# Mixture-of-experts trunk: token rows of seven experts fetched by indirect DMA and transposed, in place of one-hot products

## The chip, the cores and the metric

The kernel runs on one core of one Trainium2 chip. Its metric is the device time of one execution in microseconds, taken as the median of several runs; lower is better. Of the engines, PE (TensorE) does the matrix products, ACT (ScalarE) and DVE (VectorE) do the elementwise work, SP issues the loads, and POOL (GpSimd) is unused before the change.

## The reference

A two-layer trunk over 256 tokens of width 1024 with 256 context tokens. Layer 0 is attention and a dense SwiGLU, layer 1 is a gated convolution and a top-2-of-8 expert SwiGLU. The change lies in the last part:

```python
h = rms_norm(x, norm2_g[layer]) * (1 + sc2) + sh2
logits = (h @ router_w).astype(jnp.float32)
top_vals, top_idx = lax.top_k(logits, TOP_K)
weights = jax.nn.softmax(top_vals, axis=-1)
gates = jnp.sum(jax.nn.one_hot(top_idx, N_EXPERTS) * weights[..., None], axis=-2)
out = gates[..., 0:1] * swiglu(h, w_gate[0], w_up[0], w_down[0])
for e in range(1, N_EXPERTS):
    out = out + gates[..., e:e + 1] * swiglu(h, w_gate[e], w_up[e], w_down[e])
x = x + g2 * out
```

Each expert has three weight matrices of 1024 x 3584 in f32, 44 MB in all; eight experts make 352 MB that must come from memory.

## The kernel before, in words

The kernel ranks the experts by the number of tokens they got. The first five ranks are heavy (up to 128 tokens each), the last three are light (up to 64 tokens). Each expert's hidden width of 3584 is cut into 7 chunks of 512; a chunk needs six loads of 1 MB (two halves each of gate, up and down). The 56 chunks are processed in one fixed order, `chunks`: four heavy ones first, then heavy and light mixed about two to one, four light ones last. So expert 0 starts at step 0, expert 5 (light) at 5, expert 1 at 9, expert 2 at 20, expert 6 (light) at 25, expert 3 at 31, expert 4 at 41, expert 7 (light) at 44.

A step has twelve places p: in places 0 to 7 PE computes gate and up of its own chunk, in places 8 to 11 it computes down of the chunk before. Weights of a heavy chunk are split first: ACT rounds a half to `hi` (L71), DVE computes `lo` = raw - hi (L72), and PE makes three f32r products (L271, L273, L275). Weights of a light chunk are used as they are, in f32, two products side by side (L1319). The program order of every engine is written out by hand: `hook(n, p, f, ...)` puts a piece of work at step n, place p, and `ahead` and `feed` issue loads and conversions a few halves ahead of their use.

All loads are issued by SP, in order, into a ring of 13 buffers of 1 MB each during the experts. A load waits until the readers of the load 13 places earlier are done: the DVE subtraction for a heavy chunk, the PE product for a light one.

Before expert r starts at step n, its tokens are gathered. `choice` on DVE builds a one-hot `os` (token by slot, scaled with the token's RMS factor) at step n-3; `gather` (heavy, two groups of four column blocks, at n-1, places 5 and 8) or `gather_light` (one group, place 5) multiplies the stream `x` with it on PE in f32, which selects, scales and transposes the rows at once. `gathered` applies the modulation and splits the result. At n+2, `slots` transposes an unscaled one-hot `oh` and reads each slot's gate; `scatter` uses the transposed one after the expert's end to add its output to the tokens.

Of the kernel before, what the change touches and what calls it, by code (L numbers as in the profile page):

```python
# [24 lines left out]
CAP = 64  # L25
# [8 lines left out]
def trunk(ctx, tc, i, out, dbg=None):  # L34
    nc = tc.nc
# [22 lines left out]

    ring = [raw1] * 5

    def load(src, n=2048):
        ring.append(ring.pop(0))
        t = ring[-1].tile([128, 2048], F32, name="raw")
        sp.dma_start(t[:, :n], src)
        return t

# [70 lines left out]
    def ahead(split):  # L137

        n = used[0]
        step = 2 if whole[n // 2] else 1  # L140
        upto, k = n, n + step
        while split and k <= most[0] and k // 2 - n // 2 < 11:
            if whole[k // 2]:
                k += 2
            else:
                upto, k, split = k, k + 1, split - 1
        feed(upto)
        used[0] += step
        return ready.pop(n)

    vec = const.tile([128, 29, 8], F32, name="vec")
    cid = const.tile([128, 130], F32, name="cid")
# [1006 lines left out]
    raw5 = ctx.enter_context(pool("raw5", 1))  # L1159
    ring += [raw5]  # L1160
    me = ctx.enter_context(pool("me", 2))

    gts = m1.tile([128, NT, NE], F32, name="gts")
    posr = m1.tile([128, NT, NE], F32, name="posr")
    gtsr = m1.tile([128, NT, NE], F32, name="gtsr")
    perm = m1.tile([128, NE, NE], F32, name="perm")
    cap = m1.tile([128, NE], F32, name="cap")

# [27 lines left out]
    def by_rank(dst, src):  # L1196
        for t in range(NT):
            tmp = m1.tile([128, NE, NE], F32, name="cmp")
            dve.tensor_mul(tmp, perm, src[:, t, None, :].to_broadcast([128, NE, NE]))
            dve.reduce_sum(dst[:, t], tmp, axis=AX.X)  # L1200

    def gates():

        mx = m1.tile([128, NT], F32, name="mx")
        sm = m1.tile([128, NT], F32, name="sm")
        dve.reduce_max(mx, lg, axis=AX.X)
        dve.tensor_sub(gts, lg, mx[:, :, None].to_broadcast([128, NT, NE]))
        act.activation(gts, gts, AF.Exp)
        dve.tensor_mul(gts, gts, sl.bitcast(F32))
        dve.reduce_sum(sm, gts, axis=AX.X)  # L1210
        dve.reciprocal(sm, sm)
        dve.tensor_mul(gts, gts, sm[:, :, None].to_broadcast([128, NT, NE]))
        by_rank(gtsr, gts)
        for u in units:
            u.finish()
        dump("lg", lg)
        dump("gts", gts)
        dump("pos", pos)
# [1 line left out]
    class Expert:  # L1220
        pass

    def choice(E, pos, scaled):

        name = "os" if scaled else "oh"
        n = 2 if E.light and not scaled else 1
        w = CAP if E.light else 128
        c = me.tile([128, NT, 128], F32, name=name, bufs=1)[:, :, 0:n * w]
        for t in range(NT):
            d, io, p = c[:, t], iota[:, 0:w], pos[:, t, E.r:E.r + 1]  # L1230
            if n == 2:
                d, io = d.rearrange("p (n w) -> p n w", n=2), io[:, None, :].to_broadcast([128, 2, w])
            if scaled:
                dve.tensor_scalar(d, io, p, rs[:, t:t + 1], op0=OP.is_equal, op1=OP.mult)
            else:
                dve.tensor_scalar(d, io, p, None, op0=OP.is_equal)
        setattr(E, name, c)

    def gather_light(E):
        E.ps = pm()  # L1240
        for k in range(KD):
            for t in range(NT):
                pe.matmul(E.ps[:, k * CAP:(k + 1) * CAP], x[:, t, k * 128:(k + 1) * 128], E.os[:, t],
                          start=(t == 0), stop=(t == NT - 1))

    def gathered_light(E):
        E.h = me.tile([128, KD, CAP], F32, name="hl", bufs=1)
        w = [128, KD, CAP]
        dve.tensor_mul(E.h, E.ps.rearrange("p (k c) -> p k c", c=CAP), am[:, :, 0:1].to_broadcast(w))
        dve.tensor_add(E.h, E.h, bm[:, :, 0:1].to_broadcast(w))  # L1250
        choice(E, posr, False)

    def gather(E, ks):
        g = ks[0] // 4
# [19 lines left out]
    def gathered(E, ks, h=None):  # L1274
        h = h or modulated_rows(E, ks)
        g, ks = ks[0] // 4, slice(ks[0] % 4, ks[-1] % 4 + 1)
        act.copy(E.eh[g][:, ks], h)
        dve.tensor_sub(E.el[g][:, ks], h, E.eh[g][:, ks].bitcast(F32))
        if g and ks.stop == 4:
            choice(E, posr if E.r else pos, False)  # L1280

    def slots(E):
        E.ps = pm()
        for t in range(NT):
            pe.transpose(E.ps[:, t * 128:(t + 1) * 128], E.oh[:, t], ident)
        for t in range(NT):
            pe.matmul(E.ps[:, S:S + 1], E.oh[:, t], gtsr[:, t, E.r:E.r + 1], start=(t == 0), stop=(t == NT - 1))

    def slotted(E):
        E.ohT = me.tile([128, S], F32R, name="ohT" + "l" * E.light, bufs=2 - E.light)  # L1290
        E.gs = me.tile([128, 1], F32, name="gs" + "l" * E.light, bufs=2 - E.light)
        act.copy(E.ohT, E.ps[:, 0:S])
        act.copy(E.gs, E.ps[:, S:S + 1])

    def flip(C):
        C.ps = pm()
# [53 lines left out]
    def hook(n, p, f, *a):  # L1350
        hooks.setdefault((n, p), []).append((f, a))
# [48 lines left out]
    def down(C, s):  # L1400
# [10 lines left out]
        else:  # L1411
            k = slice(s * 128, (s + 1) * 128)
            mac(E.accs, C.dh[:, k], C.dl[:, k], *halves(ahead(4)), first, end)

    hook(0, 1, ranks)
    hook(0, 3, by_rank, posr, pos)
    hook(1, 1, gates)
    hook(3, 2, gate_rows, 1, 5, (0, 1), g2)
# [66 lines left out]
def spill(tc, i, out, load, pm, acc, me, m1, x, macc, rs, am, bm, pos, gts, cap, g2, iota, ident):  # L1485
# [4 lines left out]
        dve.tensor_sub(p2[:, t], pos[:, t], cap)  # L1490
    for e in range(NE):
        oh = me.tile([128, NT, 128], F32, name="oh", bufs=1)
        os = me.tile([128, NT, 128], F32, name="os", bufs=1)
# [58 lines left out]
def constants():  # L1552
    c = np.zeros((128, C_ATT + C_END), np.float32)
    p = np.arange(128)[:, None]
    j = np.arange(128)[None, :]
    c[:, C_TRI:C_TRI + 128] = p < j
    c[:, C_ATT + C_M0:C_ATT + C_M0 + 128] = np.where(j > p, NEG, 0.0)
    c[:, C_ATT + C_M1:C_ATT + C_M1 + 128] = np.where(j < p, NEG, 0.0)
    c[:, C_IO:C_IO + 128] = j + 1
    half = 32  # L1560
    inv = (np.float32(10000.0) ** (-np.arange(0, half, 2, dtype=np.float32) / np.float32(half))).astype(np.float32)
    t = np.arange(S)
    ang = np.concatenate([(t // 64).astype(np.float32)[:, None] * inv, (t % 64).astype(np.float32)[:, None] * inv], 1)
# [5 lines left out]
    d = np.zeros((128, 130), np.float32)  # L1569
    d[:, 0:128] = p == j  # L1570
    for r in range(2):
        d[r::32, 128 + r] = 1.0
    return c, d
# [58 lines left out]
```

## Time and profile before

| | us |
|---|---|
| three runs | 1404.34, 1409.27, 1409.58 |
| median | 1409.27 |
| profiled execution | 1407.87 |
| its span, first to last instruction | 1406.1 |
| PE busy in the span | 1375.2 (98%) |
| DVE, ACT, POOL busy | 990.2, 791.2, 0.2 |
| read from memory | 467 MB, 333 GB/s over the span |

The profiled execution's time is 1.8 us more than its span; that rest lies outside the instructions. The experts run from about 500 us to the end. A busy time is the union of an engine's instructions; since matmuls overlap, the cost of a group of them is read from the start of its first to the start of the next group.

### The profile page before, as it was taken

How to read it: one execution, taken by the hardware profiler on the slowest of the kernel's cores; microseconds unless marked ns; L12 is line 12 of the kernel's file. 1: busy time of each engine (PE TensorE's matmuls, PEld its weight loads, DVE VectorE, ACT ScalarE, POOL GpSimd, SP SyncE). 2: the span in 40 equal slices, each digit the busy share in tenths (PEclk: the TensorE clock that was granted, in tenths of full speed). 3: DMA queues.
4: the chain of work that ended last, by engine and by line, in shares of the span. 5: the costliest groups of instructions: out<-in, count | busy, mean ns of one | idle time of the engine just before them, and what ended most of it. 6: DMA issues, size and time to landing. Idle time of an engine off the chain costs nothing.

```text
span 1406.1 us, 20577 instructions
## 1 busy us (share of the span) xinstructions
PE 1375.2 (98%) x7764; PEld 1017.2 (72%) x7764; DVE 990.2 (70%) x1341; ACT 791.2 (56%) x1070; POOL 0.2 (0%) x4
## 2 busy tenths in 40 slices
PE   6999999999999999999999999999999999999997
PEld 4776789999899988776666767767667676676742
DVE  4777769788777679776766867767578667676721
ACT  5567674444463378565655755656467566465610
POOL 0000000000000000000000000000000000000000
PEclk9999999999999999999999999999999999999999
DMA  9734678678667779799899999989989999999994
GB/s 372 277 120 141 250 298 301 240 299 301 251 235 261 275 281 351 286 422 382 343 422 421 420 390 383 378 362 376 421 345 421 413 414 363 364 420 370 411 420 167
DMA packets 66060, 469.81 MB, mean 334 GB/s; under 512 B 7328, under 2 KB 7968, under 8 KB 10016
## 3 DMA queue, kind: packets, MB, share of 16 engines
q1 hardware_dynamic: 65952, 468.41, 84.2%
q8 instruction: 63, 1.03, 0.3%
q14 instruction: 45, 0.37, 0.1%
HBM read 467.33 MB, written 1.05 MB: 333 GB/s over the span
## 4 chain that ended last, share of the span: by engine, by line
PE 93%; ACT 3%; DVE 3%; issue 1%; DMA 0%; DVEq 0%; ACTq 0%
PE pm L1319 11%; PE pm L271 9%; PE pm L273 9%; PE pm L275 9%; PE acc L271 8%; PE acc L273 8%; PE acc L275 8%; PE acc L1319 5%; PE pm L927 4%; PE pm L929 4%; PE pm L928 4%; PE pm L1299 2%; PE pm L1261 2%; PE pm L181 1%; PE pm L1339 1%; PE pt L691 1%
## 5 line engine op out<-in xcount | busy, mean ns | idle before, releaser
L72 DVE TENSOR_TENSOR lo<-raw,hi 128x1024 fp32r<-128x1024 f32 x522 | 627.0, 1222 | 124.9 <-ACT hi L71 100.9
L71 ACT ACTIVATE hi<-raw 128x1024 fp32r<-128x1024 f32 x522 | 545.7, 1059 | 246.8 <-PE pm L275 113.6
L271 PE MATMUL pm<-hi,eh 128*128 128x512 f32 x560 | 224.6, 401 | 0.2
L273 PE MATMUL pm<-lo,eh 128*128 128x512 f32 x560 | 219.0, 391 | 1.8 <-DVE lo L72 1.6
L275 PE MATMUL pm<-hi,el 128*128 128x512 f32 x560 | 218.7, 391 | 0.0
L1319 PE MATMUL pm<-raw,hl 128*64 128x512 f32 x672 | 155.6, 599 | 0.0
L927 PE MATMUL pm<-th,hi 128*128 128x256 f32 x480 | 135.1, 281 | 0.0
L928 PE MATMUL pm<-tl,hi 128*128 128x256 f32 x480 | 134.6, 280 | 0.0
L929 PE MATMUL pm<-th,lo 128*128 128x256 f32 x480 | 134.6, 280 | 0.0
L271 PEld LDWEIGHTS pm<-hi,eh 128*128 128x128 f32 x560 | 105.2, 188 | 32.9 <-issue 8.8
L273 PEld LDWEIGHTS pm<-lo,eh 128*128 128x128 f32 x560 | 105.3, 188 | 24.2 <-DVE lo L72 4.1
L275 PEld LDWEIGHTS pm<-hi,el 128*128 128x128 f32 x560 | 105.1, 188 | 22.5
L1319 PEld LDWEIGHTS pm<-raw,hl 128*64 128x64 f32 x672 | 44.1, 136 | 79.8 <-issue 76.6
L927 PEld LDWEIGHTS pm<-th,hi 128*128 128x128 f32 x480 | 90.8, 189 | 1.2 <-issue 0.8
L928 PEld LDWEIGHTS pm<-tl,hi 128*128 128x128 f32 x480 | 90.7, 189 | 0.4
L929 PEld LDWEIGHTS pm<-th,lo 128*128 128x128 f32 x480 | 90.8, 189 | 0.0
L271 PE MATMUL acc<-hi,dh 128*128 128x512 f32 x280 | 88.6, 398 | 0.0
L273 PE MATMUL acc<-lo,dh 128*128 128x512 f32 x280 | 86.5, 390 | 0.0
L275 PE MATMUL acc<-hi,dl 128*128 128x512 f32 x280 | 86.3, 389 | 0.0
L1313 DVE TENSOR_TENSOR sg<-pm,sg 128x512 f32<-128x512 f32 (+1 forms) x56 | 38.5, 688 | 63.0 <-ACT sg L1312 62.7
L1319 PE MATMUL acc<-raw,dT 128*64 128x512 f32 x336 | 78.1, 600 | 0.0
L1312 ACT ACTIVATE sg<-pm 128x512 f32<-128x512 f32 (+1 forms) x56 | 32.7, 585 | 69.5 <-PE pm L1319 66.4
(323 smaller groups left out, 1639.0 us busy)
## 6 DMA issues: line engine op xcount, KB each, us to landing
raw<-in_moe_d_dram SPq DMA_DIRECT2D x112, 1024.0 KB, 10.2
raw<-in_moe_g_dram SPq DMA_DIRECT2D x111, 1024.0 KB, 9.9
raw<-in_moe_u_dram SPq DMA_DIRECT2D x111, 1024.0 KB, 9.3
raw<-in_ada_w_dram SPq DMA_DIRECT2D x48, 1024.0 KB, 6.7
raw<-in_conv_i_dram SPq DMA_DIRECT2D x12, 1024.0 KB, 6.6
raw<-in_ffn_g_dram SPq DMA_DIRECT2D x11, 1024.0 KB, 6.3
raw<-in_ffn_u_dram SPq DMA_DIRECT2D x11, 1024.0 KB, 5.1
raw<-in_ffn_d_dram SPq DMA_DIRECT2D x11, 1024.0 KB, 5.0
```

The source lines that it names most:

```text
L71: act.activation(hi, r, AF.Copy)
L72: dve.tensor_sub(lo, r, hi.bitcast(F32))
L271: pe.matmul(p, hh, wh[j], start=first, stop=False)
L273: pe.matmul(p, hh, wl[j], start=False, stop=False)
L275: pe.matmul(p, hl, wh[j], start=False, stop=last)
L927: pe.matmul(d, hi[:, c], th[:, k], start=(k == 0), stop=False)
L928: pe.matmul(d, hi[:, c], tl[:, k], start=False, stop=False)
L929: pe.matmul(d, lo[:, c], th[:, k], start=False, stop=(k == KD - 1))
L1261: pe.matmul(E.ps[:, k * 128:(k + 1) * 128], x[:, t, kk * 128:(kk + 1) * 128], E.os[:, t], start=(t == 0), stop=(t == NT - 1))
L1312: act.activation(sg, C.g, AF.Silu)
L1313: dve.tensor_mul(sg, C.u, sg)
L1319: pe.matmul(ps[m * CAP:(m + 1) * CAP], lhsT, w, start=first, stop=last, tile_position=(0, m * CAP))
```

## The change

The stream `x` (1 MB) is stored to a buffer `xd` in memory early in the experts (step 1). For experts 1 to 7 the one-hot `oh` is built at n-3 and goes through `slots` at n-2 instead of n+2. `slots` now multiplies it with three columns: the gate, the RMS factor and the token's number. From the third, as an integer, an indirect DMA on POOL's queue fetches the expert's rows (128 of 4 KB, or 64) from `xd` into a buffer taken from the ring of loads, at step n-2, place 4. ACT scales the rows in place at (n-1, 2), and PE transposes them at the places where the gather products stood. Expert 0 keeps the products. `ahead` looks 9 loads ahead at most instead of 11.

```diff
+    def spare():
+        ring.append(ring.pop(0))
+        return ring[-1].tile([128, 2048], F32, name="raw")
     def load(src, n=2048):
-        ring.append(ring.pop(0))
-        t = ring[-1].tile([128, 2048], F32, name="raw")
+        t = spare()
         sp.dma_start(t[:, :n], src)
...
-        while split and k <= most[0] and k // 2 - n // 2 < 11:
+        while split and k <= most[0] and k // 2 - n // 2 < 9:
...
-        by_rank(gtsr, gts)
+        by_rank(slotv[:, :, :, 0], gts)
+        for t in range(NT):
+            dve.tensor_copy(slotv[:, t, :, 1], rs[:, t:t + 1].to_broadcast([128, NE]))
+            dve.tensor_scalar(slotv[:, t, :, 2], cid[:, 130:131].to_broadcast([128, NE]), 128.0 * t, None, op0=OP.add)
...
+    def fetch_rows(E):
+        E.idx = me.tile([128, 1], I32, name="idx")
+        dve.tensor_copy(E.idx, E.v[:, 2:3])
+        w = CAP if E.light else 128
+        E.xg = spare()[0:w, 0:D]
+        nc.gpsimd.indirect_dma_start(out=E.xg, out_offset=None, in_=xd[:, :],
+                                     in_offset=bass.IndirectOffsetOnAxis(ap=E.idx[0:w, 0:1], axis=0))
+    def scale_rows(E):
+        act.activation(E.xg, E.xg, AF.Copy, scale=E.v[0:E.xg.shape[0], 1:2])
+    def turn_rows(E, ks):
+        ...
+        w = E.xg.shape[0]
         E.ps = pm()
-        for k in range(KD):
-            for t in range(NT):
-                pe.matmul(E.ps[:, k * CAP:(k + 1) * CAP], x[:, t, k * 128:(k + 1) * 128], E.os[:, t], ...)
+        for k, kk in enumerate(ks):
+            pe.transpose(E.ps[:, k * w:(k + 1) * w], E.xg[:, kk * 128:(kk + 1) * 128], ident[0:w, 0:w])
...
-            pe.matmul(E.ps[:, S:S + 1], E.oh[:, t], gtsr[:, t, E.r:E.r + 1], start=(t == 0), stop=(t == NT - 1))
+            pe.matmul(E.ps[:, S:S + 3], E.oh[:, t], slotv[:, t, E.r], start=(t == 0), stop=(t == NT - 1))
...
-            hook(n - 3, 10, choice, E, posr, True)
+            hook(n - 3, 10, choice, E, posr)
+            hook(n - 2, 2, slots, E)
+            hook(n - 2, 3, slotted, E)
+            hook(n - 2, 4, fetch_rows, E)
+            hook(n - 1, 2, scale_rows, E)
             if E.light:
-                hook(n - 1, 5, gather_light, E)
+                hook(n - 1, 5, turn_rows, E, range(KD))
...
-                    hook(n - 1, (5, 8)[g], gather, E, ks)
+                    hook(n - 1, (5, 8)[g], turn_rows, E, ks)
...
-        hook(n + 2, 2, slots, E)
-        hook(n + 2, 3, slotted, E)
...
+    def store_rows():
+        for t in range(NT):
+            sp.dma_start(xd[t * 128:(t + 1) * 128, :], x[:, t])
+    hook(1, 0, store_rows)
```

## Rows read from the trace of the kernel before

**Rows 1.** The page's first part: busy time, share of span, instructions of each engine.

```profile
PE 1375.2 (98%) x7764; PEld 1017.2 (72%) x7764; DVE 990.2 (70%) x1341; ACT 791.2 (56%) x1070; POOL 0.2 (0%) x4
```

**Rows 2.** Windows: stretch, its length, busy time by engine, clock, DMA share, GB/s.

```profile
600.00:1375.00 775.00, 773.21 (x3549) 515.07 (x3550) 529.58 (x524) 447.18 (x521) 0.00 (x0) 1.00 0.97 394
700.00:725.00 25.00, 25.00 (x116) 14.82 (x114) 15.86 (x14) 13.01 (x14) 0.00 (x0) 1.00 1.01 422
525.00:550.00 25.00, 25.00 (x117) 20.73 (x116) 24.59 (x25) 21.75 (x25) 0.00 (x0) 1.00 0.95 358
```

**Rows 3.** Waits from 480 us on: who waited for whom, total, times, longest.

```profile
PEld pm L273 <- DVE lo L72: 4.1, 6, 1.0
PEld pm L1319 <- DMA raw<-in_moe_d_dram: 0.9, 3, 0.3
...
SPq L64 <- DVE lo L72: 384.3, 151, 11.4
SPq L64 <- PE pm L1319: 190.9, 39, 9.6
```

**Rows 4.** Timeline of PE at expert 1's gather: start, length, line, tiles, count.

```profile
640.84 2.05 PE L1261 MATMUL pm<-os,x 128*128 128x128 f32 x16
642.82 2.79 PE L1319 MATMUL pm<-raw,hl 128*64 128x512 f32 x12
645.55 2.05 PE L1261 MATMUL pm<-os,x 128*128 128x128 f32 x16
647.36 0.71 PE L271 MATMUL acc<-hi,dh 128*128 128x512 f32 x2
```

**Rows 5.** Timeline of PE at expert 7's gather and 19 us before it.

```profile
1186.49 2.79 PE L1319 MATMUL pm<-raw,hl 128*64 128x512 f32 x12
...
1205.95 3.68 PE L1243 MATMUL pm<-os,x 128*128 128x64 f32 x32
1209.44 0.48 PE L271 MATMUL pm<-hi,eh 128*128 128x512 f32 x1
```

**Rows 6.** Timeline of PE at transposes of hidden tiles: 128 rows twice, 64 rows once.

```profile
520.70 0.60 PE L1299 MATMUL pm<-cid,sg 128*128 128x128 f32 x4
521.05 0.48 PE L271 MATMUL pm<-hi,eh 128*128 128x512 f32 x1
...
606.93 0.46 PE L1299 MATMUL pm<-cid,sg 64*128 64x64 f32 x4
607.32 0.50 PE L271 MATMUL pm<-hi,eh 128*128 128x512 f32 x1
...
638.39 0.66 PE L1299 MATMUL pm<-cid,sg 128*128 128x128 f32 x4
638.97 1.94 PE L1319 MATMUL pm<-raw,hl 128*64 128x512 f32 x8
```

**Rows 7.** Groups by shape: busy, mean ns of one, idle before, releaser.

```profile
L71 ACT ACTIVATE hi<-raw 128x1024 fp32r<-128x1024 f32 x522 | 545.7, 1059 | 246.8 <-PE pm L275 113.6 <-PE pm L928 64.7 <-PE acc L275 56.1
L1234 DVE TENSOR_SCALAR os<-cst,posr,rs 128x128 f32<-128x128 f32 x8 | 2.4, 340 | 0.0
```

**Rows 8.** Timeline of PE around expert 3's gather, from step 29, place 4.

```profile
980.42 0.39 PE L271 MATMUL pm<-hi,eh 128*128 128x512 f32 x1
...
994.57 2.05 PE L1261 MATMUL pm<-os,x 128*128 128x128 f32 x16
```

**Rows 9.** DMA: x's loads (KB each, median us to landing); L64's loads, min/median/max.

```profile
x<-in_x_dram SPq DMA_DIRECT2D x2, 512.0 KB, 4.5
...
DMA to landing us min/median/max: 4.7/8.9/15.8
```

**Rows 10.** Timeline of SP's issues around expert 1's fetch; then a use on PE.

```profile
597.69 0.86 SPq L64 DMA_DIRECT2D raw<-in_moe_d_dram  x2
...
625.39 3.54 SPq L64 DMA_DIRECT2D raw<-in_moe_d_dram  x2
...
665.81 1.94 PE L1319 MATMUL acc<-raw,dT 128*64 128x512 f32 x8
```

More of the change, by code (lines that the diff above doesn't have):

```diff
@@ L151, in trunk @@
     vec = const.tile([128, 29, 8], F32, name="vec")
-    cid = const.tile([128, 130], F32, name="cid")
+    cid = const.tile([128, 131], F32, name="cid")
     cst = const.tile([128, C_ATT], F32, name="cst")
@@ L1161, in trunk @@
     me = ctx.enter_context(pool("me", 2))
+    xd = ctx.enter_context(tc.tile_pool(name="xd", bufs=1, space=bass.MemoryType.DRAM)).tile([S, D], F32, name="xd")
     gts = m1.tile([128, NT, NE], F32, name="gts")
     posr = m1.tile([128, NT, NE], F32, name="posr")
-    gtsr = m1.tile([128, NT, NE], F32, name="gtsr")
+    slotv = m1.tile([128, NT, NE, 3], F32, name="slotv")
     perm = m1.tile([128, NE, NE], F32, name="perm")
@@ L1221, in trunk @@
         pass
-    def choice(E, pos, scaled):
-        name = "os" if scaled else "oh"
-        n = 2 if E.light and not scaled else 1
-        w = CAP if E.light else 128
-        c = me.tile([128, NT, 128], F32, name=name, bufs=1)[:, :, 0:n * w]
-        for t in range(NT):
[L1230 to L1237, printed above, removed]
@@ L1239, in gather_light, with choice @@
-    def gather_light(E):
+    def choice(E, pos, scaled=False):
+        n = 2 if E.light else 1
+        if scaled:
+            c = E.os = me.tile([128, 512], F32, name="dl", bufs=1)[:, 0:S].rearrange("p (t c) -> p t c", t=NT)
+        else:
+            c = E.oh = me.tile([128, NT, 128], F32, name="oh", bufs=1)
+        for t in range(NT):
+            d, io = (v.rearrange("p (n w) -> p n w", n=n) for v in (c[:, t], iota))
+            if n == 2:
+                io = iota[:, None, 0:CAP].to_broadcast([128, 2, CAP])
+            if scaled:
+                dve.tensor_scalar(d, io, pos[:, t, E.r:E.r + 1], rs[:, t:t + 1], op0=OP.is_equal, op1=OP.mult)
+            else:
+                dve.tensor_scalar(d, io, pos[:, t, E.r:E.r + 1], None, op0=OP.is_equal)
@@ new lines, in fetch_rows @@
+    def fetch_rows(E):
+        E.idx = me.tile([128, 1], I32, name="idx")
+        dve.tensor_copy(E.idx, E.v[:, 2:3])
+        w = CAP if E.light else 128
+        E.xg = spare()[0:w, 0:D]
[4 more added lines that the diff above has]
+    def turn_rows(E, ks):
+        g = ks[0] // 4
+        if not E.light:
+            E.eh[g] = me.tile([128, 4, 128], F32R, name=f"eh{g}", bufs=1)
+            E.el[g] = me.tile([128, 4, 128], F32R, name=f"el{g}", bufs=1)
+        w = E.xg.shape[0]
@@ L1240, in gather_light @@
         E.ps = pm()
-        for k in range(KD):
-            for t in range(NT):
-                pe.matmul(E.ps[:, k * CAP:(k + 1) * CAP], x[:, t, k * 128:(k + 1) * 128], E.os[:, t],
-                          start=(t == 0), stop=(t == NT - 1))
+        for k, kk in enumerate(ks):
+            pe.transpose(E.ps[:, k * w:(k + 1) * w], E.xg[:, kk * 128:(kk + 1) * 128], ident[0:w, 0:w])
     def gathered_light(E):
@@ L1250, in gathered_light @@
         dve.tensor_add(E.h, E.h, bm[:, :, 0:1].to_broadcast(w))
-        choice(E, posr, False)
     def gather(E, ks):
@@ L1278, in gathered @@
         dve.tensor_sub(E.el[g][:, ks], h, E.eh[g][:, ks].bitcast(F32))
-        if g and ks.stop == 4:
-            choice(E, posr if E.r else pos, False)
     def slots(E):
@@ L1286, in slots @@
         for t in range(NT):
-            pe.matmul(E.ps[:, S:S + 1], E.oh[:, t], gtsr[:, t, E.r:E.r + 1], start=(t == 0), stop=(t == NT - 1))
+            pe.matmul(E.ps[:, S:S + 3], E.oh[:, t], slotv[:, t, E.r], start=(t == 0), stop=(t == NT - 1))
     def slotted(E):
-        E.ohT = me.tile([128, S], F32R, name="ohT" + "l" * E.light, bufs=2 - E.light)
-        E.gs = me.tile([128, 1], F32, name="gs" + "l" * E.light, bufs=2 - E.light)
+        E.ohT = me.tile([128, S], F32R, name="ohT" + "l" * E.light)
+        E.v = me.tile([128, 3], F32, name="gs" + "l" * E.light)
+        E.gs = E.v[:, 0:1]
         act.copy(E.ohT, E.ps[:, 0:S])
-        act.copy(E.gs, E.ps[:, S:S + 1])
+        act.copy(E.v, E.ps[:, S:S + 3])
     def flip(C):
@@ L1370, in trunk @@
                     ks = range(4 * g, 4 * g + 4)
-                    hook(n - 1, (5, 8)[g], gather, E, ks)
+                    hook(n - 1, (5, 8)[g], turn_rows, E, ks)
                     hook(n - 1, (6, 9)[g], gathered, E, ks)
-        hook(n + 2, 2, slots, E)
-        hook(n + 2, 3, slotted, E)
+        else:
+            hook(2, 1, choice, E, pos)
+            hook(2, 2, slots, E)
+            hook(2, 3, slotted, E)
         if end < len(chunks) - 1:
@@ L1413, in down @@
             mac(E.accs, C.dh[:, k], C.dl[:, k], *halves(ahead(4)), first, end)
+    def store_rows():
+        for t in range(NT):
+            sp.dma_start(xd[t * 128:(t + 1) * 128, :], x[:, t])
     hook(0, 1, ranks)
+    hook(1, 0, store_rows)
     hook(0, 3, by_rank, posr, pos)
@@ L1492, in spill @@
         oh = me.tile([128, NT, 128], F32, name="oh", bufs=1)
-        os = me.tile([128, NT, 128], F32, name="os", bufs=1)
+        os = me.tile([128, 4, 128], F32, name="el0", bufs=1)
         for t in range(NT):
@@ L1568, in constants @@
     c[:, C_LT8:C_LT8 + 64] = (e[None, :] < e[:, None]).reshape(1, 64)
-    d = np.zeros((128, 130), np.float32)
+    d = np.zeros((128, 131), np.float32)
+    d[:, 130] = np.arange(128)
     d[:, 0:128] = p == j
```

## The prediction

> **What bounds the kernel now.** I read the page's first part for the busiest engine, then windows for its pace inside the experts, then the waits, then PE's timeline at the places that the change touches. PE is busy for 98% of the span [rows 1], and from 600 to 1375 us for 773.2 of 775 us at full clock [rows 2]. A busy PE can still hide waits, so I looked at who waits for whom: PE's own waits for conversions come to 4.1 us in six places and for a load to 0.9 us [rows 3]. SP, on the other hand, waits hundreds of microseconds for buffers to come free (384.3 us for the subtraction on DVE, 190.9 us for light products) [rows 3]. So loads run ahead as far as the ring lets them, and PE's own work sets the end. What leaves PE's queue shortens the time one for one, as long as the engines that feed PE keep up. Two of them are near their limit. In the first heavy steps DVE is busy 24.59 of 25 us [rows 2]. And memory delivers 394 GB/s over the long window, where a saturated window shows 422 [rows 2]: of 775 us some 775 x (1 - 394/422) = 51 us of transfer time are unused.
>
> **The products removed.** Expert 1 (heavy) shows the pattern. Its first group runs from 640.84 to the next product at 642.82, its second from 645.55 to 647.36: 1.98 + 1.81 = 3.79 us [rows 4]. The other heavy experts do the same work; 4 x 3.79 = 15.2 us. A light expert has one group, for expert 7 from 1205.95 to 1209.44: 3.49 us [rows 5], three times 10.5 us. Removed: 25.6 us. Expert 0 keeps its own.
>
> **The transposes added.** They have the shape of the transposes of hidden tiles. Four of 128 rows take 521.05 - 520.70 = 0.35 us between f32r products and 638.97 - 638.39 = 0.59 us between light ones; four of 64 rows take 0.39 us [rows 6]. A heavy expert needs two groups of four (0.70 to 1.18 us; I take 1.06, since three of the four stand in light steps), a light one eight of 64 rows (0.39 to 0.78 us; I take 0.65, the entry being paid once). That is 4 x 1.06 + 3 x 0.65 = 6.2 us, between 4.0 and 7.1. PE's net: 25.6 - 6.2 = 19.4 us less, between 18.5 and 21.6.
>
> **Parts that cost PE nothing.** `slots` moves from n+2 to n-2 with the same instructions; its products write three columns instead of one, and next to 128 columns per transpose that can't be seen. Scaling the rows on ACT has the shape of a conversion, 1059 ns [rows 7]; seven of them are 7.4 us on an engine that is busy 447 of 775 us [rows 2]. DVE loses the scaled one-hots (two instructions of 340 ns per heavy expert [rows 7], shorter ones per light expert) and gains seven small integer copies and four small table instructions: about even. Counting through `feed` and `ahead` over the fixed list of chunks, the look-ahead never reaches the ninth load before it has its four or five halves, so 9 instead of 11 gives the same order of loads and conversions: nothing.
>
> The store of `x` stands in SP's queue, two issues and 1 MB, that is 1.05 MB / 422 GB/s = 2.5 us of transfer. The loads of step 3 queue behind it. The DMA has slack there (358 GB/s [rows 2]) and the loads are issued far ahead of use, so I cost it at nothing; without that cover it is 2.5 us, once.
>
> **What the removed time covered.** While PE multiplied one-hots, DVE and ACT went on converting. Of the gathers, those of experts 4, 5, 6 and 7 stand in heavy steps, where DVE has the least to spare. PE will reach the next `lo` sooner there. The six waits that exist cost 0.7 us each [rows 3]; I expect two more, 1.4 us. Ends: none, or the whole gain in those steps (second rival). Sum: 19.4 - 1.4 = 18.0 us.
>
> **The fetch.** No row of before shows an indirect DMA or POOL at work. Its landing matters at one place: `scale_rows` at (n-1, 2) waits on ACT, and behind it in ACT's queue stand the `hi` conversions and the copies that PE needs; the transposes on PE wait for it too. The tightest is expert 3. Step 29, place 4, begins on PE at 980.42 and the gather at 994.57 [rows 8]: 14.2 us, less 1.06 us for scaling and about 1 us for the integer copy and its handover, leaves 12 us from issue to landing. The widest is expert 7: place 4 of step 42 lies four products into the group at 1186.49, so at about 1187.4, and its gather at 1205.95 [rows 5]: 18.5 us, 16.5 left. The same two places of the other five lie 16.2 to 18.2 us apart, 14 to 16 left. The nearest rows for the price are a plain load of the same 512 KB, 4.5 us, and the slowest load of 1 MB in a full queue, 15.8 us [rows 9]. I take 6 to 9 us, nearer the low end: the size is that of the first row, but the queue is as full as in the second. Then the fetch is hidden.
>
> Here the Trainium skill speaks against the change. Its page "SBUF — State Buffer" (section "SBUF: two separate sides") says that descriptors of a POOL DMA are written by GpSimd through a port that some DVE instructions hold exclusively, and calls it a trap: the DMA then waits for descriptors. Here DVE holds long two-input subtractions nearly back to back. No row of before can show whether it happens; if it did, the time would be that of the third rival, and without it that of the sum.
>
> **The ring.** The fetch takes one of the 13 ring buffers, and holds it from the turn at which a load would have had it until the transposes at n-1. For expert 1 that turn is just before the loads issued at 597.69, and the load 13 places on is one issued at 625.39 [rows 10]. That load, and by SP's order all behind it, now waits for the second group of transposes, at about 645.55 - 1.5 + 0.4 = 644.4 [rows 4]: 19 us later than before. Earlier loads have landed by 625.4 + 8.9 = 634 [rows 9], so the DMA lies idle for about 9 us. Is it hidden? The load is first needed at 665.81 [rows 10], 3 us sooner in the changed kernel, and would land at 644.4 + 4.7 = 649.1 [rows 9]: 13.7 us to spare. So PE doesn't see one such hole. The seven fetches move 2.75 MB, 2.9 MB / 422 GB/s = 7 us.
>
> **The rivals.**
>
> First, the loads become the bound. The DMA has 51 us unused [rows 2]; a PE that is 18 us faster and the fetches take 25 of them, which leaves 26. Seven holes of 9 us would be 63. Against it: a DMA that is already late has loads in flight when SP is stuck, so the hole shrinks as the lag grows and settles near 9 us, inside the 13.7 us. For it: light steps need data faster than the DMA delivers. If the lag passes the 13.7 us, the excess (63 - 26 - 13.7 = 23 us) comes through in part. With half of it 12 us of the 18 are lost: about 1402; with all of it 1414.
>
> Second, conversions become the bound where gathers stood in heavy steps. Then the gains of experts 5, 6, 7 (3.49 - 0.65 each) and of 4 (2.7) are lost: 11.2 us, the sum is 8.2, the time 1400. For it speaks DVE's 24.59 of 25 us; against it, that this holds only at the beginning, while over the long window DVE is busy 530 of 775 us [rows 2].
>
> Third, slower than before: the fetch lands late. The place is ACT's queue at `scale_rows`. The price is the sum over the seven of latency minus what is left to each (12 for expert 3, 14 for 1 and 2, 14.4 for 4 and 6, 16 for 5, 16.5 for 7). At 15.8 us that is 3.8 + 3.6 + 2.8 = 10 us, time 1401. At 17 us it is 18 us and the change is worth nothing: from there it is slower, by 7 us for each further microsecond. At 20 us it costs 39 and gives 1430. For it: the path through POOL is unknown here and the load queue is full. Against it: 512 KB need no more than 1.2 us of transfer at 422 GB/s.
>
> Fourth, the change does what it says but PE's time is given back in places that I can't name: no change, 1409.
>
> **How the numbers follow.** The profiled execution took 1407.87 us, so 1407.87 - 18.0 = 1389.9; it lies 1.4 us under the median of the runs, 1409.27, from which the sum gives 1391.3. I say 1390.5. Chances: forecast (1384 to 1398) 0.70; loads 0.10; conversions 0.08; fetch late 0.10, of which 0.08 slower than before; no change 0.02. The low end takes the upper bound of PE's net, 21.6 us, without new waits, from the fastest of the runs shown back to the profile: 1407.87 - 21.6 = 1386, and 1 us for the runs' spread: 1385. The high end takes in the second rival and the milder half of the first and third: 1403. A change under 0.5% (7 us) can't be told from none here. Faster by more than that, under 1402.2: 0.70 + 0.08 + half of the loads, 0.83. Within: the other half, 0.02 of the late fetch and the no change, 0.09. Slower: 0.08.
>
> **What would show it.** In the changed kernel: L1261 only for expert 0 and none of L1243; new transposes of 0.35 to 0.6 us per four; PE still busy over 99% between 600 and 1360 us, with the clock at full speed; fetches that land within 12 us of their issue; ACT without waits for the fetch at `scale_rows`. Wrong would be: waits of ACT or PE for the fetched rows (third rival), PE waiting for loads with the DMA at 422 GB/s all the time (first), or PE waiting for `lo` just after the transposes of experts 4 to 7 (second).

## The result: 0.6% faster, under half of the forecast

| | before | after |
|---|---|---|
| median of the runs | 1408.88 us (14 runs) | 1400.86 us (14 runs) |
| lowest and highest | 1404.34 to 1411.99 | 1394.20 to 1404.53 |
| profiled execution, its span | 1407.87, 1406.1 | 1398.09, 1396.2 |
| PE, DVE, ACT busy | 1375.2, 990.2, 791.2 | 1359.2, 987.4, 798.3 |

The ratio after to before is 0.9939, with a 95% interval from 0.9924 to 0.9954 (one execution of after, 1933 us at a mean granted clock of 0.653, is left out here and in the table). That is 8 to 9 us of gain; 18 us were forecast, and 1390.5 us named. The time lies inside the stated range of 1385 to 1403 us, but the gain is less than half of the forecast.

Line numbers of the changed kernel: products of heavy weights L274, L276, L278; conversions L74 (`hi`, ACT) and L75 (`lo`, DVE); one-hots L1245; indirect DMA L1253; scaling L1257; transposes L1267; `slots` L1305 and L1307; flip of hidden tiles L1320; scatter of an expert's outputs L1360; light products L1340; store of `x` L1444. `dl` is written at two places: the scaled one-hot of expert 0 (L1243) and the low part of a flipped hidden tile (L1329). In the runs e2, e5, e6 and e8 to e11 lines from the indirect DMA on stand two further down, in e7 those from the transposes on twelve further up; b1 has the numbers of before.

The page's busy times and its DMA queues, of after:

```profile
PE 1359.2 (97%) x7596; PEld 997.2 (71%) x7596; DVE 987.4 (71%) x1338; ACT 798.3 (57%) x1077; POOL 10.3 (1%) x11
...
q0 software_dynamic: 816, 2.88, 0.6%
```

PE does 16.0 us less than in [rows 1], with 168 instructions fewer; the fetches have a queue of their own and move 2.88 MB (2.9 in the forecast). The window over the experts (length, busy time by engine, clock, DMA share, GB/s), of after:

```profile
600.00:1365.00 765.00, 759.19 (x3405) 499.10 (x3405) 527.00 (x518) 453.39 (x526) 8.27 (x6) 1.00 0.98 405
```

In [rows 2] PE left 1.8 of 775 us idle; here it leaves 5.8 of 765. So PE is still busy for 99% of that stretch, as the prediction's signs asked for, with half of the gain missing: the share does not show it. Small holes have come. The waits of PE from 480 us on tell where (who waits for whom, total, times, longest), of after:

```profile
PE pm L276 <- DVE lo L75: 2.0, 4, 0.5
PE pm L1360 <- DVE dl L1329: 1.7, 1, 1.7
PE pm L1305 <- DVE oh L1245: 1.6, 1, 1.6
PE pm L1320 <- DVE sg L1334: 1.5, 1, 1.5
...
PE pm L1267 <- ACT raw L1257: 0.7, 1, 0.7
```

The waits for `lo` have hardly changed. The row to compare with is PE's own of before; the 4.1 us in six of [rows 3] are those of PEld, the weight loads, which overlap PE's products. PE's row of before, then PEld's row of after:

```profile
PE pm L273 <- DVE lo L72: 1.6, 3, 0.5
```

```profile
PEld pm L276 <- DVE lo L75: 4.5, 6, 1.0
```

Three single waits of 1.5 to 1.7 us are new: at expert 0's `slots`, at a flip, and at a scatter of expert outputs. A fourth, of 0.7 us, is that for the scaled rows.

To see what each costs I set PE's timelines of two kernels side by side at the first product of every step: the start in the one kernel minus the start in before. Where this difference falls, the change gains; where it rises, it loses. Counted from step 0 on, after gains 9.15 us by the last step. The table shows the change of that difference over three of the 56 steps (from the first product of the step to that of the next) for every kernel but e11, and the sum over all:

```
us against before          step 2   step 13  step 24   step 0 to end
after                       +3.45    +1.61    +1.45       -9.15
e1  one-hot early            0.00    +1.55    +1.43      -12.72
e2  ring tile late          +3.42     0.00    -0.18      -12.66
e3  store by ACT            +3.47    +1.62    +1.45       -9.12
e4  scaling first           +1.85    +1.57    +0.54      -11.76
e5  e1+e2+e4                 0.00     0.00    +0.61      -15.28
e6  e5 + scatters moved      0.00     0.00    -2.35      -18.29
e7  PE part alone           +3.40     0.00    -1.03      -13.34
e8  e6 without e4            0.00     0.00    -1.51      -17.43
e9  e5 again                 0.00     0.00    -0.99      -16.85
e10 e6 again                 0.00     0.00    -2.38      -18.07
b1  before, one-hot late    +1.84     0.00     0.00       +1.93
```

Everywhere else the steps of after behave as forecast: the gathers of experts 5, 1, 2, 3, 4 and 7 gain 2.80, 2.76, 2.79, 2.77, 2.65 and 3.45 us. At step 24 (expert 6) it should have been -2.35, as in e6, and it is +1.45. So three holes cost 3.45 + 1.61 + 3.80 = 8.9 us of PE's time, nearly all of the 9.1 us that part 9.15 from 18.29.

**The hole at step 2.** Timeline of PE, of after (start, length, line, tiles, count, idle before):

```profile
535.60 0.39 PE L278 MATMUL pm<-hi,el 128*128 128x512 f32 x1
537.62 0.43 PE L1305 MATMUL pm<-cid,oh 128*128 128x128 f32 x2 [1.62 <-DVE oh L1245]
537.89 0.51 PE L1307 MATMUL pm<-slotv,oh 128*128 128x3 f32 x4
...
539.17 0.63 PE L274 MATMUL pm<-hi,eh 128*128 128x512 f32 x1
539.60 0.63 PE L276 MATMUL pm<-lo,eh 128*128 128x512 f32 x1
540.03 0.63 PE L278 MATMUL pm<-hi,el 128*128 128x512 f32 x1
```

Timeline of DVE in the same stretch, of after:

```profile
533.77 3.50 DVE L75 TENSOR_TENSOR lo<-raw,hi 128x1024 fp32r<-128x1024 f32 x3
537.18 0.49 DVE L1245 TENSOR_SCALAR oh<-cst,pos 128x128 f32<-128x128 f32 x2
```

PE comes to expert 0's `slots`, and its one-hot stands in DVE's queue behind three `lo`. The change builds that one-hot at (2, 1), one place ahead of its use; before, it was built right after expert 0's gather, and PE went through `slots` with no wait (timeline of PE, of before):

```profile
536.43 0.38 PE L1285 MATMUL pm<-cid,oh 128*128 128x128 f32 x2
```

In after, from 538.80 on, the products start 0.43 us apart in place of 0.23: that is the lower of the clock's two levels, 1.2 in place of 2.4 GHz. Windows of after:

```profile
535.00:540.00 5.00, 3.38 (x16) 2.56 (x15) 4.93 (x7) 2.23 (x4) 0.00 (x0) 0.89 0.93 346
540.00:545.00 5.00, 5.00 (x21) 4.05 (x19) 2.37 (x3) 2.85 (x4) 0.00 (x0) 0.77 0.84 277
```

The granted clock is 0.89 and 0.77, so 5 x 0.11 + 5 x 0.23 = 1.7 us are lost beside the wait.

**The hole at step 13.** Timeline of SP's issues, of after:

```profile
626.60 0.33 SPq L67 DMA_DIRECT2D raw<-in_moe_u_dram  x1
645.46 0.91 SPq L67 DMA_DIRECT2D raw<-in_moe_d_dram  x2
```

For 18.9 us SP issues nothing: the next load's tile is held by expert 1's fetched rows until their transposes at 645.37. Windows of after, the two stretches behind that:

```profile
625.00:650.00 25.00, 25.00 (x116) 16.29 (x114) 15.73 (x17) 17.64 (x26) 1.76 (x1) 1.00 0.74 297
650.00:675.00 25.00, 24.39 (x108) 16.92 (x107) 21.72 (x23) 16.66 (x20) 0.00 (x0) 1.00 1.01 422
```

The DMA is idle for a quarter of 25 us and then full (419 to 422 GB/s in every 25 us up to 800 us). Timeline of ACT, then of PE, of after:

```profile
711.40 2.01 ACT L74 ACTIVATE hi<-raw 128x1024 fp32r<-128x1024 f32 x2 [5.66 <-DMA raw<-in_moe_d_dram]
```

```profile
719.48 0.66 PE L1320 MATMUL pm<-cid,sg 128*128 128x128 f32 x4 [1.52 <-DVE sg L1334]
```

Sixty microseconds later ACT waits 5.66 us for a load, the conversions queue up, the hidden tile behind them is late, and PE waits for it.

**The hole at step 24.** Timeline of PE at expert 6's transposes, of after:

```profile
894.89 0.39 PE L278 MATMUL pm<-hi,el 128*128 128x512 f32 x1
896.00 0.71 PE L1267 MATMUL pm<-cid,raw 64*128 64x64 f32 x8 [0.73 <-ACT raw L1257]
896.64 0.50 PE L274 MATMUL pm<-hi,eh 128*128 128x512 f32 x1
...
897.90 0.40 PE L278 MATMUL pm<-hi,el 128*128 128x512 f32 x1
900.04 0.47 PE L1360 MATMUL pm<-yh,ohTl 64*128 64x512 f32 x1 [1.74 <-DVE dl L1329]
```

Here ACT has stood 7.57 us for an output tile and then has the output's cast, conversions, the scaling and the copy of a turned hidden tile to do, in that order. PE waits 0.73 us for the scaling, and 1.74 us for the PSUM bank that `dl` empties. Slow products follow; the window behind it, of after, has a granted clock of 0.66:

```profile
900.00:905.00 5.00, 4.96 (x14) 3.77 (x15) 4.86 (x6) 2.24 (x3) 0.00 (x0) 0.66 1.02 418
```

### The profile page after: what moved, and what is told of

Same layout as the page of the kernel before. It is cut to its first block, busy times and chain, and to the rows that moved or that the text cites. A ratio compares the mean times of both kernels' runs of the same rounds, so it can differ in the third digit from the quotient of the medians.

```text
span 1396.2 us, 20283 instructions
## 1 busy us (share of the span) xinstructions
PE 1359.2 (97%) x7596; PEld 997.2 (71%) x7596; DVE 987.4 (71%) x1338; ACT 798.3 (57%) x1077; POOL 10.3 (1%) x11
## 3 DMA queue, kind: packets, MB, share of 16 engines
q0 software_dynamic: 816, 2.88, 0.6%
## 4 chain that ended last, share of the span: by engine, by line
PE 88%; DVE 5%; ACT 4%; DMA 2%; issue 1%; SPq 0%; ACTq 0%; DVEq 0%
PE pm L1340 11%; PE pm L274 9%; PE pm L276 8%; PE pm L278 8%; PE acc L274 8%; PE acc L276 7%; PE acc L278 7%; PE acc L1340 4%; PE pm L930 4%; PE pm L931 4%; PE pm L932 4%; PE pm L1320 2%; DVE lo L75 2%; DMA raw<-in_moe_g_dram 1%; ACT hi L74 1%
## 5 line engine op out<-in xcount | busy, mean ns | idle before, releaser
L75 DVE TENSOR_TENSOR lo<-raw,hi 128x1024 fp32r<-128x1024 f32 x522 | 627.0, 1224 | 135.8 <-ACT hi L74 113.1
L74 ACT ACTIVATE hi<-raw 128x1024 fp32r<-128x1024 f32 x522 | 546.2, 1061 | 246.0 <-PE pm L278 107.5
L274 PE MATMUL pm<-hi,eh 128*128 128x512 f32 x560 | 226.0, 404 | 0.4 <-ACT g L260 0.2
L276 PE MATMUL pm<-lo,eh 128*128 128x512 f32 x560 | 220.3, 393 | 2.1 <-DVE lo L75 2.0
L278 PE MATMUL pm<-hi,el 128*128 128x512 f32 x560 | 219.6, 392 | 0.0
L1340 PE MATMUL pm<-raw,hl 128*64 128x512 f32 x672 | 155.4, 599 | 0.0
L274 PEld LDWEIGHTS pm<-hi,eh 128*128 128x128 f32 x560 | 105.8, 189 | 33.9 <-issue 8.0
L276 PEld LDWEIGHTS pm<-lo,eh 128*128 128x128 f32 x560 | 106.0, 189 | 24.7 <-DVE lo L75 4.5
L278 PEld LDWEIGHTS pm<-hi,el 128*128 128x128 f32 x560 | 105.8, 189 | 22.8
L1340 PEld LDWEIGHTS pm<-raw,hl 128*64 128x64 f32 x672 | 44.1, 136 | 80.6 <-issue 77.9
L274 PE MATMUL acc<-hi,dh 128*128 128x512 f32 x280 | 88.7, 398 | 0.0
L276 PE MATMUL acc<-lo,dh 128*128 128x512 f32 x280 | 86.5, 390 | 0.0
L278 PE MATMUL acc<-hi,dl 128*128 128x512 f32 x280 | 86.3, 389 | 0.0
L1340 PE MATMUL acc<-raw,dT 128*64 128x512 f32 x336 | 78.1, 600 | 0.0
```

Source lines behind the costliest of these rows:

```text
L74: act.activation(hi, r, AF.Copy)
L75: dve.tensor_sub(lo, r, hi.bitcast(F32))
L274: pe.matmul(p, hh, wh[j], start=first, stop=False)
L276: pe.matmul(p, hh, wl[j], start=False, stop=False)
L278: pe.matmul(p, hl, wh[j], start=False, stop=last)
L1340: pe.matmul(ps[m * CAP:(m + 1) * CAP], lhsT, w, start=first, stop=last, tile_position=(0, m * CAP))
```

## The experiments

My theory after reading the trace was that of separate holes: the sum of the forecast holds, and three short waits with a cause each, together with slow products behind two of them, took half of it back. The rivals were that SP's stand at the store of `x` costs the loads their lead and makes all three, or that fetch and scaling as such do it.

The ratio of each to before, 95% interval in brackets, and the median:

| run | ratio | median us |
|---|---|---|
| after | 0.9939 [0.9924, 0.9954] | 1400.86 |
| e1_choice0 | 0.9908 [0.9884, 0.9933] | 1396.65 |
| e2_late_tile | 0.9926 [0.9906, 0.9947] | 1398.68 |
| e3_store_act | 0.9944 [0.9922, 0.9966] | 1401.91 |
| e4_scale_first | 0.9935 [0.9913, 0.9958] | 1399.69 |
| e5_three / e9_three_again | 0.9869 [0.9850, 0.9887] / 0.9865 [0.9850, 0.9880] | 1389.05 / 1390.08 |
| e6_four / e10_four_again | 0.9869 [0.9850, 0.9888] / 0.9865 [0.9842, 0.9888] | 1388.82 / 1391.94 |
| e7_pe_alone | 0.9917 [0.9897, 0.9937] | 1397.75 |
| e8_no_scale | 0.9878 [0.9863, 0.9893] | 1391.89 |
| e11_fetch_late | 1.0162 [1.0142, 1.0181] | 1434.69 |
| b1_choice0_late | 1.0015 [1.0003, 1.0026] | 1410.91 |

**Expert 0's one-hot early.**

```diff
-            hook(2, 1, choice, E, pos)
             hook(2, 2, slots, E)
...
             gathered(experts[0], ks[n], hs[n])
+    choice(experts[0], pos)
```

> The changed kernel with expert 0's one-hot built where the kernel before built it, right after expert 0's gather, and not one place ahead of its slots at (2, 1). Theory 'separate holes' (the gain is lost in three short holes of PE with a cause each): PE's wait of 1.6 us for that one-hot at 535 to 538 us and the slow matmuls behind it (some 2.5 us at half clock) go, so 4 us less, about 1396.5 us. Theory 'store' (SP's stand of 23 us at the store of x takes the loads' lead, and everything later follows from it): the hole only moves to the next use, and the time stays within 1 us of 1400.9.

Measured: 4.2 us below after in the medians; the intervals of the two ratios still overlap a little, so it is the trace that decides. In the table the loss of 3.45 us at step 2 is gone, and the other two holes are unchanged. The wait for `oh` is no longer among PE's waits, and the clock stays at 1.00 from 510 us to 900 us.

**The ring tile taken later.**

```diff
+    def fetch_dma(E):
         w = CAP if E.light else 128
         E.xg = spare()[0:w, 0:D]
...
             hook(n - 2, 4, fetch_rows, E)
+            hook(n - 1, 0, fetch_dma, E)
```

> The changed kernel with the indirect DMA, and with it its tile of the ring, taken one step's place later in program order, at (n - 1, 0) where it was (n - 2, 4); the row numbers are still made at (n - 2, 4), so that the fetch can start when it did. Theory 'separate holes': SP's waits for the transposes' tile fall from 58 us to under 20, the loads of expert 5's step come in time, and the hole at step 13 goes: 1.6 to 2.5 us less, 1398.5 us. Theory 'store': SP's waits fall too, but the time stays at 1400.9.

Measured: 2.2 us below after in the medians, within the spread of both, but the trace is plain. SP's waits for the transposes' tile from 450 us on, of after and then of e2 (under 20 us had been expected):

```profile
SPq L67 <- PE pm L1267: 58.2, 5, 15.8
```

```profile
SPq L67 <- PE pm L1269: 24.0, 3, 11.0
```

The hole at step 13 is gone (0.00 in the table), and ACT's wait for the load with it. In e2 the wait for `dl` at step 24 is still there, 1.7 us, but this time no slow products follow; that alone turns the +1.45 there into -0.18.

**The store issued by ACT.**

```diff
-            sp.dma_start(xd[t * 128:(t + 1) * 128, :], x[:, t])
+            act.dma_start(xd[t * 128:(t + 1) * 128, :], x[:, t])
```

> The changed kernel with the two stores of x issued by ACT in place of SP, at the same place of the program. SP then passes the place without a stand. Theory 'store': DMA's share between 475 and 500 us goes back from 0.36 to about 0.9, the holes at steps 2 and 13 go, and with them 6 to 8 us: 1393 to 1395 us. Theory 'separate holes': the loads come earlier, but PE's holes stay where they are: within 1.5 us of 1400.9.

Measured: no gain over after, 1401.91 us, and all three holes as they were. SP's stand at the store is real (waits of SP from 450 us on, of after):

```profile
SPq L1444 <- DVE x L833: 22.8, 1, 22.8
```

and the edit takes it away. The window of after, and then that of e3:

```profile
475.00:500.00 25.00, 24.16 (x158) 20.08 (x157) 14.32 (x34) 10.26 (x25) 0.00 (x0) 0.89 0.36 135
```

```profile
475.00:500.00 25.00, 24.26 (x161) 20.14 (x159) 13.28 (x34) 9.56 (x23) 0.00 (x0) 0.89 0.84 331
```

The DMA has its share back, and the time does not care. The theory of the store falls.

**The scaling ahead of the output's cast.**

```diff
-            hook(n - 1, 2, scale_rows, E)
+            hook(n - 1, 0, scale_rows, E)
```

> The changed kernel with ACT's scaling of the fetched rows at (n - 1, 0), ahead of the output's cast at (n - 1, 1), where it was (n - 1, 2), behind it. Theory 'separate holes': at step 24 (expert 6) ACT has the scaling done while it waits 7.6 us for the output, the transposes and the scatter behind them wait less, and 2.5 to 4 us of that hole go: 1397.5 us. Theory 'fetch late': ACT waits longer for the rows (5.4 us at expert 3 before), the conversions behind it are late, and the time rises by up to 5 us. Theory 'store': no change, 1400.9.

Measured: 1399.69 us, no difference that these runs can tell. In the trace step 24 loses 0.91 us less; PE's wait for the scaling is gone, that for `dl` is still 1.5 us. Expected were 2.5 to 4 us: too much. The hole at step 2 is instructive here. PE waits the same 1.65 us, and no slow products follow; the window with that wait, of e4:

```profile
540.00:545.00 5.00, 3.35 (x21) 2.70 (x20) 4.26 (x6) 2.28 (x5) 0.00 (x0) 1.00 0.87 298
```

The clock is 1.00, and the loss is 1.85 us in place of 3.45. So the slow stretch costs 1.6 us where it comes, and it does not always come.

**Three edits together, then four.** The fourth moves the scatters one place back:

```diff
-                hook(end + 2 + m // 2, (6, 10)[m % 2], scatter, E, q, t)
-                hook(end + 2 + m // 2, (8, 11)[m % 2], scattered, E, q, t)
+                hook(end + 2 + m // 2, (7, 10)[m % 2], scatter, E, q, t)
+                hook(end + 2 + m // 2, (9, 11)[m % 2], scattered, E, q, t)
```

> The changed kernel with three of the single edits together: expert 0's one-hot built early, the ring tile of the fetch taken later, the scaling ahead of the output's cast. Theory 'separate holes': the parts add up, 3.5 to 4 us at step 2, 1.6 us at step 13, about 1 us at step 24, so 6 to 6.5 us below the changed kernel's 1400.9: 1394.5 us. Theory 'one lead' (the holes share the conversions' lead, and what one edit gives the next hole takes): no better than the best single edit, 1396.7 us.

> The three edits, and the scatters of the experts' outputs at places 7 and 10 of a step in place of 6 and 10 (their additions at 9 and 11), so that at step 24 expert 5's scatter doesn't stand right behind expert 6's transposes and doesn't wait for the PSUM bank that ACT and DVE empty late. Theory 'separate holes': what is left of the hole at step 24 (a wait of 1.5 us and some matmuls at half clock) goes too: 2 to 3 us below the three edits, about 1392 us. Theory 'conversions' (the hole at step 24 is the conversions' own lateness once the gather's products don't cover them): the wait moves to the next products, and the time is that of the three edits.

> The kernel with the three edits once more, beside the one with four on the same chip. Each hole's own price says 1.5 to 3 us more than with four; the first comparison gave no difference (1389.1 and 1388.8 us). If the spread comes from the granted clock of the first step, the medians of enough runs differ by 1.5 us or more.

> The kernel with the four edits once more, beside that with three: 1387 to 1388 us, and 1.5 us or more below that with three, if the hole at step 24 is worth what its trace says.

Measured: 0.9869 and 0.9865 with three, the same with four. The parts add up and rather more: 18.4 to 19.0 us below before, against 8 to 9 of after, so the interval of after is left far behind. The traces with three edits gain only 6.1 and 7.7 us over that of after from step 0 on, where the ratios say about 10. The rest is not in these traces. It goes with the mean granted clock of the single runs (0.990 to 0.998 in after, 0.994 to 0.999 with three edits), and part of it lies ahead of step 0, whose first product starts between 2.4 us earlier and 4.3 us later than in before, from trace to trace. The forecast has no term for it. In the trace the fourth edit closes the hole at step 24 (PE's waits from 480 us on, of e6):

```profile
PE pm L276 <- DVE lo L75: 2.1, 5, 0.5
...
PE pm L1362 <- DVE dl L1331: 0.2, 1, 0.2
```

From step 0 to the end e6 gains 18.29 us and the repeat 18.07; with three edits it is 15.28 (e5), where slow products follow the wait at step 24, and 16.85 (e9), where they don't. In the medians the fourth edit can't be told from none (in the second comparison four stand 1.9 us above three): the runs of one kernel spread over 3 to 8 us, with the mean granted clock between 0.992 and 0.999. The expected 1.5 us stays open as a difference of times.

**Without the scaling's edit.** It is the four edits less one (`scale_rows` stays at (n - 1, 2)).

> Expert 0's one-hot early, the ring tile late and the scatters moved, but ACT's scaling left at (n - 1, 2), behind the output's cast. Theory 'order on ACT' (the hole at step 24 is made by the scaling's place): 0.7 us and perhaps a stretch of half clock come back at step 24, 1390 us. Theory 'scatter' (it is made by the scatter's wait for the PSUM bank alone): the same time as with four edits, 1388.8 us.

Measured: 0.9878, not to be told from 0.9869 or 0.9865. At step 24 it gains 1.51 in place of 2.35 us, so 0.8 us hang on the scaling's place, as the trace of after says (0.73).

**The TensorE part alone.**

```diff
-            hook(n - 2, 4, fetch_rows, E)
-            hook(n - 1, 2, scale_rows, E)
+            E.xg = x[0:CAP if E.light else 128, 0]
...
-    hook(1, 0, store_rows)
```

> The change's TensorE part alone: no store of x, no fetch, no tile of the ring, no scaling; the transposes turn rows of x as they lie in SBUF (the rows are not the experts' own, so this part of the computation is left out). Theory 'separate holes': the hole at step 2 stays (1.6 us of wait and its clock), that of step 13 goes (1.6 us) as no tile is held, that of step 24 stays but for the 1 us of scaling: 2 to 3 us below the changed kernel, 1398 us. Theory 'fetch' (all that was lost was lost to fetch, store and scaling): the 18 us of the forecast appear, 1390 us.

Measured: 1397.75 us, 3 us below after with intervals that overlap, and not the 1390 us at which fetch and scaling would be to blame. In the traces it gains 13.34 us: fetch, held tile and scaling together account for 4.2 of the 9.1 us that after lacks (1.6 of it slow products at step 24, which come and go), and the rest comes without them. The hole at step 13 is gone, as no tile is held. The hole at step 2 is there with 3.40 us, and PE's wait at step 24 too (waits of PE from 885 to 910 us, of e7):

```profile
PE pm L1348 <- DVE dl L1317: 1.5, 1, 1.5
```

With neither fetch nor scaling PE still waits for `dl`: what made that place tight is most likely the 3.5 us of products that were taken from it. (The moved `slots` are in e7 too; no run takes them out.)

**The kernel before, with the one-hot late.**

```diff
-        if g and ks.stop == 4:
+        if g and ks.stop == 4 and E.r:
...
+        if not r:
+            hook(2, 1, choice, E, pos, False)
```

> The kernel before with one piece of the change: expert 0's one-hot is built at (2, 1), one place ahead of its slots, as in the changed kernel. Theory 'separate holes': PE waits about 1.6 us for it there, with or without matmuls at half clock behind it: 1.6 to 4 us more than before, about 1411 us. If that hole needs the rest of the change: no difference, 1408 us.

Measured: 1.0015 [1.0003, 1.0026], 2 us slower, and 1.93 us by the trace. The wait comes alone, without the rest of the change (waits of PE from 480 us on, of b1):

```profile
PE pm L1285 <- DVE oh L1236: 1.6, 1, 1.6
```

**The fetch made late.**

```diff
-            hook(n - 2, 4, fetch_rows, E)
+            hook(n - 1, 0, fetch_rows, E)
```

> The first kernel of this batch with the row numbers made at (n - 1, 0) in place of (n - 2, 4), so that each fetch starts eight places, some 14 to 16 us, later. This is the prediction's rival 'fetch late' brought about: it said that up to about 17 us of fetch hide. With 8.4 us to landing and 15 us of delay the rows come some 6 us too late: by that rival ACT stands for the rows in its order, conversions queue behind it, and PE loses 2 to 5 us at each of seven fetches, 1403 to 1424 us. If there is more cover than the rival said, under 1395 us.

Measured: 1434.69 us, 42.8 us above the same kernel without this edit (e8), and above the upper end of what I had expected, 1424. The first two fetches on POOL, of e8 and then of e11:

```profile
562.81 1.81 POOL L1255 DMA_INDIRECT raw<-xd,idx  x1 [562.35 <-DVE dl L1331]
625.46 1.85 POOL L1255 DMA_INDIRECT raw<-xd,idx  x1 [60.84 <-DVE dl L1331]
```

```profile
576.81 1.28 POOL L1255 DMA_INDIRECT raw<-xd,idx  x1 [576.36 <-DMA raw<-in_moe_d_dram]
647.11 1.37 POOL L1255 DMA_INDIRECT raw<-xd,idx  x1 [69.01 <-ACT hi L74]
```

They start 14.0 and 21.7 us later, of which 3.7 and 10.3 us are e11's own lag by then (PE's timelines at the first product of steps 4 and 8): 10 to 11 us against the work around them, less than the 14 to 16 I had expected. Waits of ACT, then of PE, from 480 us on, of e11:

```profile
ACT raw L1259 <- DMA raw<-xd,idx: 48.6, 7, 11.9
```

```profile
PE pm L1269 <- ACT raw L1259: 26.7, 7, 6.0
```

All seven fetches are late, ACT stands in its order for each, PE waits 26.7 us, and the mean granted clock falls to 0.979 (0.997 in e8). How the other 16 us split between slow products and conversions that came late behind ACT's stand was not separated.

## Why the prediction failed, and what of it held

- **Products out, transposes in: right.** Four transposes of 128 rows take 642.64 - 642.06 = 0.58 and 645.78 - 645.37 = 0.41 us, 0.99 in place of 1.06; eight of 64 rows 896.64 - 896.00 = 0.64, in place of 0.65. Timeline of PE at expert 1's transposes, of after:

```profile
642.06 0.66 PE L1267 MATMUL pm<-cid,raw 128*128 128x128 f32 x4
642.64 2.79 PE L1340 MATMUL pm<-raw,hl 128*64 128x512 f32 x12
645.37 0.66 PE L1267 MATMUL pm<-cid,raw 128*128 128x128 f32 x4
645.78 0.71 PE L274 MATMUL acc<-hi,dh 128*128 128x512 f32 x2
```

  The seven gathers of e6 gain 2.76, 2.80, 2.80, 2.35, 2.80, 2.70 and 3.43 us, together 19.6; the forecast said 19.4. The moved `slots` give and take 0.7 to 1.1 us at a time and cost about 1 us in all. Another 0.35 us go at step 1, for which no cause was looked for. Once the holes are closed the whole is 18.3 us on PE. The 18.4 to 19.0 of the runs agree with that partly by luck, since three edits show the same with 15.3 to 16.9 on PE. The sum was right; what stood against it was left out or too small.
- **"Parts that cost PE nothing" is the step that failed first.** I listed the move of `slots`, but not that expert 0's one-hot moves too, from the end of its gather to (2, 1). It is in the whole diff, on the line ahead of expert 0's `slots`: `hook(2, 1, choice, E, pos)`. In this very stretch I had read DVE as busy for 24.59 of 25 us [rows 2]: an instruction put one place ahead of its use behind a full queue is a wait. Cost: 1.85 us, 3.45 with the slow products.
- **"What the removed time covered": right in kind, wrong in place and size.** I took two more waits for `lo` of 0.7 us, 1.4 in all. The price was read from the wrong row: 4.1 us in six are PEld's, and PE itself waited 1.6 us in three. It now waits 2.0 in four, 0.4 us more. The wait came at one of the places that the second rival named, the light expert 6 in a heavy step, but as a wait for a PSUM bank (1.74 us) and for the scaling (0.73), with slow products behind: 3.8 us of gain lost in place of 1.4. Experts 4, 5 and 7, which that rival named too, lost nothing.
- **The ring: the hold was right, the spare was not.** A stand of 19 us for the load that follows expert 1's fetch was forecast, and 18.9 us measured. But the 13.7 us to spare were those of the load that waited. The DMA runs full for the next 150 us, so the lag is passed on from load to load, and it comes out 60 us later at a load with less to spare. This is the first rival in one place: 1.6 us.
- **The store: nothing, as said, with a wrong reason.** The cost isn't 2.5 us of transfer in a queue; SP reaches the store before `x` is done and stands there for 22.8 us, and the loads behind it too. e3 shows that this costs nothing here.
- **The fetch: hidden, as said.** Landing of the seven fetches of after, by the view of the indirect DMA's line:

```profile
L1253 POOL DMA_INDIRECT raw<-xd,idx x7: 908/1754/1993, 564.8 to 1185.7; - x7
...
DMA to landing us min/median/max: 4.9/8.4/11.2
```

  I took 6 to 9 us, nearer the low end, with 12 to spare at the tightest; the median is 8.4, and three of the seven take 9.2 to 11.2 us. ACT waits 5.4 us once, at expert 3, where I had named any such wait as a sign against me; it cost PE nothing, and that gather gains 2.77 us like the others. The third rival's arithmetic has the right order but is too small: 8.4 + 10.5 = 19 us of fetch would have cost 18 + 2 x 7 = 32 us by it; e11 shows 26.7 us of PE's waits and 42.8 us in all.

  The exclusive use that spoke against the change does show, at a size that the landing covers. Timelines of DVE and then of POOL, of after:

```profile
980.18 1.23 DVE L75 TENSOR_TENSOR lo<-raw,hi 128x1024 fp32r<-128x1024 f32 x1 [0.69 <-ACT hi L74]
```

```profile
980.23 1.99 POOL L1253 DMA_INDIRECT raw<-xd,idx  x1 [99.42 <-ACT hi L74]
...
1132.51 0.94 POOL L1253 DMA_INDIRECT raw<-xd,idx  x1 [150.28 <-DMA raw<-in_moe_d_dram]
```

  The instruction at 980.23 starts in a subtraction that has 1.18 us left, and takes 1.99 us; that at 1132.51 finds none, and takes 0.94. In all the traces it is so: 0.91 to 0.94 us where no subtraction runs or one has begun less than 0.1 us before, and elsewhere the rest of the subtraction plus 0.78 to 0.91 us (five fetches of e11 find 0.38 to 0.55 us left and take 1.28 to 1.37). The port rule of the Trainium skill's page "SBUF — State Buffer" (section "SBUF: two separate sides") is that a DVE instruction with two SBUF inputs holds a port pair against a GpSimd operation that reads SBUF, as this one reads its row numbers, and the one that starts second waits for the other's end. The trace agrees in these numbers, though POOL's times are rough and no run takes the subtractions away. It costs up to 1.1 us of a fetch that lands in 4.9 to 11.2, with DVE busy 69% of the long window, and PE sees nothing of it.
- **Left out altogether: the clock.** I priced a wait at its length. After the idle 1.62 us at step 2, and 0.73 and 1.74 us at step 24, the products often ran at the lower level for 3 to 4 us, 1.6 us more for each.

## What to carry to other kernels

When PE is busy 98% of the time, list every instruction that a diff moves, also the small ones on other engines, and ask of each how long the queue ahead of it is where it now stands; a one-hot of 0.5 us cost 1.85 to 3.45 us, while seven fetches landed without PE noticing. A buffer that is held longer is not paid for by the load that waits for it but by the tightest load behind it, if the DMA has no slack to catch up. And when a change takes long work off the bounding engine, look for what fills the place: here three edits of order, without any change of the work, about doubled the gain.

## What the runs showed of the chip

- The same PE idle time of 1.6 us is followed by slow products in some executions (after) and not in others (e4, b1), at 1.6 us a time. Besides, there is a slow stretch at about 495 to 505 us (granted clock 0.50 from 495 to 500 us in after, 0.63 in before), which in some runs is not there at all (1.00 in e6 and e9). The spread of the times follows the mean granted clock: executions of after with a mean granted clock of 0.998 took 1394.2 us, those with 0.990 about 1404.
- An indirect DMA of 64 or 128 rows of 4 KB lands in 8.4 us at the median and 4.9 at best, in a kernel whose plain loads of twice that size have a median of 13 us in the full queue. The Trainium skill's page "DMA: Bandwidth & Descriptors" (section "Anatomy of one DMA — SWDGE (gpsimd) path") gives 2.0 us and the bytes at 436 GB/s, an estimate of 2.6 us for 64 rows and 3.2 for 128; no fetch here was that fast.
